# A decoder layer's attention probabilities, turned by VectorE's 32x32 block transposes and a way over DRAM instead of by TensorE

## The chip, the cores and the metric

The kernel runs on one core of a Trainium2 chip. The core has five engines, each with its own queue of instructions that it works through strictly in order: TensorE (PE, matrix products, with the weight loads shown as PEld), VectorE (DVE), ScalarE (ACT), GpSimd (POOL) and SyncE (SP, which here only issues DMA transfers). They wait for each other by semaphores. Data lies in the on-chip memory SBUF (128 partitions), in PSUM (the matrix products' accumulators, in banks of 128 x 512 floats) or in DRAM. The metric is the device time of one execution in microseconds (us); less is better. The kernel before takes 956.22 us, the median of three runs from 954.28 to 958.12.

## The reference

One layer of a hybrid decoder over 1024 tokens with 16 learned meta tokens ahead of them, width 1024, everything in float32:

```python
u = rmsnorm(h, g_pre_mix); z = u @ w_in            # q | k | v | x_rec | y_rec
attn = sliding_window_attention_with_sinks(q, k, v, sinks)   # 8 heads of 64, 2 KV heads, window 128
rec  = gelu(y_rec) * rg_lru(causal_conv4(x_rec))             # a gated linear recurrence over time
h = h + rmsnorm(concat(attn, rec) @ w_out, g_post_mix)
u = rmsnorm(h, g_pre_ffn)
h = h + rmsnorm(relu(u @ w_ff1)**2 @ w_ff2, g_post_ffn)
```

The attention part is the one that the change touches. For a block of 128 query tokens a head looks at 256 keys (its own block and the block before), of which each query may see 128; one more score per head, the sink, takes part in the denominator alone:

```python
s = where(valid, q @ k.T * scale, -1e30)
m = maximum(max(s), sink);  p = exp(s - m);  denom = sum(p) + exp(sink - m)
o = (p / denom) @ v
```

The product with v needs the probabilities with the keys in the partitions, while softmax leaves them with the queries in the partitions. So each 128 x 128 block of probabilities has to be turned.

## The kernel before

Every float32 product is made of three products of rounded parts (a high part and the rest, `hi` and `lo`): `split` writes `hi` with a ScalarE cast (line 96) and `lo` with a VectorE subtraction (line 99), and `mm3` issues the three matmuls (lines 125, 130, 131). Matmuls of that form are most of TensorE's work, in every stage.

The stages in time: load and normalise the tokens and project the first columns (to about 60 us), attention together with the remaining input projections (about 60 to 190 us), the recurrence (LRU; about 190 to 260 us), the output projection, and from about 300 us the feed-forward part.

Attention runs in eight steps, a loop over `j` (4 pairs of heads) and `half` (the first or second 512 query tokens). A step handles two heads `h` and four blocks of 128 queries each:

- `scores(j, half, q)`: for each head 8 matmuls into two PSUM banks of the tag `s` (lines 625, 629); ScalarE copies one half of them to the tile `sn` (line 642), VectorE overwrites it with the other half where the mask says so (line 643), so that each query keeps just the 128 keys it may see; a minimum over the row (line 652), four exponentials with their sums (line 82, the helper `lut`), a reciprocal and a multiplication (lines 660, 661).
- `attend(j, half, sn)`: TensorE turns four 128 x 128 blocks per head through the PSUM tag `pt` (line 675); `split` writes `ph` and `pl` from PSUM; eight `affine_select` on GpSimd (line 680) cut each of them into the two key blocks; 10 + 10 matmuls with v (line 691); the two heads' halves are added (lines 705, 706) into a piece called `flat` of the tile that came in, and split into the operand `at` of the output projection.

`attend` of a step is written behind `scores` of the next one. Between them stands `next_fill()`: one more input projection ("fill"), 48 or 96 matmuls into the two PSUM banks of the tag `acc`, which keep TensorE busy while softmax runs elsewhere. Fills are q, x and y projections; their results leave the banks by ScalarE and VectorE (lines 476 and 479 for q, 490 for x, 747 for y). There are ten fills: eight in the loop, two after the gates of the recurrence.

The order on each engine's queue is not the order of the program text. A planner, run when the kernel is built, simulates the program with its own costs and places each instruction by priority when its inputs are ready in that simulation; fills have their priority put back by `FILL_LAG`, so that they fill holes. What comes out is one fixed list per engine. On the chip each engine keeps to its list and waits where an input is late.

SBUF tiles come from slots: `slot(tag, ...)` takes the next buffer of a tag, and a new tile waits until the earlier tile in its buffer has been used up. The tag `c` has 8 buffers (`bufs`), and attention's `sn`, `ph` and `pl` all lie there: 5 tiles in each step (one `sn`, two `ph`, two `pl`). The PSUM tags have two buffers each.

The recurrence (`gates`, `gather`, `decay`, `recur`, `rec_out`) is a chain through TensorE (gate products, line 817), ScalarE (sigmoid, then exp, tanh, sqrt and gelu, each set with a table load) and VectorE (a scan, line 851). While it runs, TensorE has the last fills and the part of the output projection that needs attention alone (`out_mm` with `kc` 0 to 3); `kc` 4 to 7 need the recurrence.

The issue of nearly all loads is on SP, in one list; it waits at a load whose buffer is not yet free, and what stands behind it waits too.

## Time and profile before

| what | value |
|---|---|
| median of three runs | 956.22 us (954.28 to 958.12) |
| span of the profiled execution | 955.3 us (the page gives no other time for it) |
| TensorE (PE) busy | 943.8 us, 99% |
| VectorE busy | 655.7 us, 69% |
| ScalarE busy | 505.9 us, 53% |
| GpSimd busy | 129.1 us, 14% |
| TensorE transposes of line 675 | 64, first at 80.9 us, last at 175.4 us |
| matmuls with v, line 691 | 87.6 to 185.3 us |
| first gate product, line 817 | 196.6 us |

The profile is one execution recorded by the hardware. A group row gives line, engine, operation, the tile written and the tiles read (buffer numbers left out), the count, and behind the bar the busy time in us, the mean of one in ns and the idle time of the engine ahead of the group with what ended it. A timeline row gives the start in us, the length in us, the engine, the line, the operation and, in brackets, the idle time ahead of it. Matmuls overlap in the array, so the distance between two starts says what one of them costs, not its length.

### The profile page before, as it was taken

The page shows a single profiled execution, that of the slowest core. Times are in us where ns is not written, and L with a number is a line of the kernel's source. Part 1 is how long each engine was busy: PE and PEld are TensorE (multiplying, and loading weights), DVE is VectorE, ACT ScalarE, POOL GpSimd, SP SyncE. Part 2 cuts the span into 40 slices and gives each one's busy share as a digit, 9 for nine tenths or more (in the row PEclk, how much of TensorE's full clock was granted, in tenths as well). Part 3 has the DMA queues.
Part 4 walks back from the last instruction along what each step waited for, and adds up shares of the span by engine and source line. Part 5 has one row for each costly group of instructions (what it writes and reads, how often), then busy time and mean ns, then how long its engine had stood idle before and what let it go on. Part 6 is the DMA issues. An engine that isn't in the chain of part 4 may idle for free.

```text
span 955.3 us, 12432 instructions
## 1 busy us (share of the span) xinstructions
PE 943.8 (99%) x4728; PEld 789.7 (83%) x4728; DVE 655.7 (69%) x845; ACT 505.9 (53%) x854; POOL 129.1 (14%) x189
## 2 busy tenths in 40 slices
PE   9999999999999999999999999999999999999996
PEld 8999999877888878888888888888887788888885
DVE  6567987788856787665644465476667576779893
ACT  7537766568645554444655575654433343446441
POOL 4102563520021100010000000001121100001201
PEclk9999999999999999999999999999999999999999
DMA  8221010204226368674422364334777765647934
GB/s 271 56 67 23 24 45 24 67 23 131 83 109 185 133 220 264 198 253 144 155 89 88 111 203 127 104 113 114 175 180 186 185 199 177 192 139 196 246 65 89
DMA packets 88199, 130.21 MB, mean 136 GB/s; under 512 B 13702, under 2 KB 52630, under 8 KB 88140
## 3 DMA queue, kind: packets, MB, share of 16 engines
q1 hardware_dynamic: 78972, 104.44, 34.0%
q0 software_dynamic: 8880, 24.19, 12.2%
q8 instruction: 37, 0.61, 0.3%
q10 hardware_dynamic: 288, 0.79, 0.2%
q14 instruction: 22, 0.18, 0.1%
HBM read 109.93 MB, written 18.87 MB: 135 GB/s over the span
## 4 chain that ended last, share of the span: by engine, by line
PE 88%; DVE 5%; ACT 3%; DMA 2%; POOL 1%; issue 1%; SPq 0%; DVEq 0%; ACTq 0%; POOLq 0%
PE ps_acc L130 10%; PE ps_acc L131 10%; PE ps_acc L125 10%; PE ps_s L131 6%; PE ps_s L130 6%; PE ps_s L125 6%; PE ps_pt L130 6%; PE ps_pt L131 6%; PE ps_pt L125 6%; PE ps_o L130 5%; PE ps_o L131 5%; PE ps_o L125 5%; ACT c L82 1%; PE ps_o L691 1%; PE ps_acc L282 1%
## 5 line engine op out<-in xcount | busy, mean ns | idle before, releaser
L99 DVE TENSOR_TENSOR ws<-raw,ws 128x1024 fp32r<-128x1024 f32 (+1 forms) x69 | 82.6, 1197 | 76.1 <-ACT ws L96 24.3
L96 ACT CAST ws<-raw 128x1024 fp32r<-128x1024 f32 (+1 forms) x68 | 69.7, 1026 | 87.9 <-PE ps_o L130 23.9
L96 ACT CAST ws<-e 128x1024 fp32r<-128x1024 f32 x41 | 43.0, 1049 | 82.8 <-PE ps_o L130 35.3
L125 PE MATMUL ps_acc<-a,ws 128*128 128x256 f32 (+2 forms) x256 | 85.8, 335 | 0.0
L130 PE MATMUL ps_acc<-a,ws 128*128 128x256 f32 (+2 forms) x256 | 85.5, 334 | 0.0
L131 PE MATMUL ps_acc<-a,ws 128*128 128x256 f32 (+2 forms) x256 | 85.0, 333 | 0.0
L99 DVE TENSOR_TENSOR b<-b,b 128x1024 fp32r<-128x1024 f32 (+2 forms) x50 | 58.9, 1177 | 24.8 <-PE ps_o L130 19.1
L96 ACT CAST b<-b 128x1024 fp32r<-128x1024 f32 (+2 forms) x49 | 49.9, 1019 | 46.4 <-DVE b L996 41.0
L99 DVE TENSOR_TENSOR ws<-e,ws 128x1024 fp32r<-128x1024 f32 x41 | 50.1, 1223 | 32.4 <-ACT ws L96 18.9
L680 POOL TENSOR_SCALAR_AFFINE_SELECT c<-c 128x512 fp32r<-128x512 f32 x64 | 53.6, 858 | 67.6 <-ACT c L96 59.3
L125 PEld LDWEIGHTS ps_acc<-a,ws 128*128 128x128 f32 x256 | 48.3, 189 | 4.7 <-issue 0.2
L131 PEld LDWEIGHTS ps_acc<-a,ws 128*128 128x128 f32 x256 | 48.3, 189 | 4.5
L130 PEld LDWEIGHTS ps_acc<-a,ws 128*128 128x128 f32 x256 | 48.2, 188 | 4.4 <-issue 0.4
L125 PE MATMUL ps_acc<-ws,b 128*128 128x512 f32 (+1 forms) x120 | 46.3, 387 | 1.1 <-ACT ws L96 1.1
L130 PE MATMUL ps_acc<-ws,b 128*128 128x512 f32 (+1 forms) x120 | 46.3, 386 | 0.5 <-DVE ws L99 0.4
L131 PE MATMUL ps_acc<-ws,b 128*128 128x512 f32 (+1 forms) x120 | 46.1, 385 | 0.0
L125 PE MATMUL ps_pt<-ws,b 128*128 128x512 f32 x112 | 44.4, 396 | 0.0
L130 PE MATMUL ps_pt<-ws,b 128*128 128x512 f32 x112 | 44.1, 394 | 0.0
L131 PE MATMUL ps_pt<-ws,b 128*128 128x512 f32 x112 | 44.0, 393 | 0.0
L125 PE MATMUL ps_s<-ws,b 128*128 128x512 f32 x110 | 43.4, 395 | 0.0
L131 PE MATMUL ps_s<-ws,b 128*128 128x512 f32 x110 | 43.3, 394 | 0.0
L130 PE MATMUL ps_s<-ws,b 128*128 128x512 f32 x110 | 43.3, 393 | 0.0
(416 smaller groups left out, 2662.0 us busy)
## 6 DMA issues: line engine op xcount, KB each, us to landing
raw<-in_w_ff_dram SPq DMA_DIRECT2D x61, 512.0 KB, 4.1
e<-in_w_ff_dram SPq DMA_DIRECT2D x45, 512.0 KB, 4.0
a<-in_w_ff_dram SPq DMA_DIRECT2D x12, 512.0 KB, 6.6
s_dram<-a POOLq DMA_DIRECT2D x12, 512.0 KB, 3.7
c<-in_x_dram SPq DMA_DIRECT2D x8, 512.0 KB, 4.0
raw<-in_w_in_dram SPq DMA_DIRECT2D x8, 512.0 KB, 3.7
d<-in_x_dram SPq DMA_DIRECT2D x8, 512.0 KB, 3.3
out_dram<-raw SPq DMA_DIRECT2D x8, 512.0 KB
```

The lines of the kernel that those rows point to most:

```text
L82: ins = nc.scalar.activation(*args, **kwargs).ins
L96: nc.scalar.copy(hi, src)
L99: low = nc.vector.tensor_tensor(lo, src, f32(hi), op=ALU.subtract).ins
L125: ins = nc.tensor.matmul(dst, lh, rh, start=start, stop=False, skip_group_check=True).ins
L130: nc.tensor.matmul(dst, lh, rl, start=False, stop=False, skip_group_check=True)
L131: last_mm[0] = nc.tensor.matmul(dst, ll, rh, start=False, stop=stop, skip_group_check=True).ins.name
L282: last_mm[0] = nc.tensor.matmul(acc[:, :n], w[k // 2][:, kc, :], u[kc][k % 2][:, t0 : t0 + n], start=k == 0 and kc == 0, stop=k == last an ...
L680: nc.gpsimd.affine_select(out=p_[:, :, s], in_=f32(p_[:, :, 0]), pattern=[[0, 4], [g, P]], compare_op=op, fill=0.0, base=0, channel_multip ...
L691: nc.tensor.matmul(po[:, oc : oc + n], v, p_[:, pc : pc + n], start=first and k == 0, stop=last and k == 1, skip_group_check=True,)
```

## The change

`scores` no longer returns `sn`. Behind the multiplication it runs one VectorE transpose per step, which turns each 32 x 32 block of `sn` by itself and writes a new tile `y` of the tag `c`. Four DMAs on SP, one for each group of 32 partitions, write `y` to a DRAM tile `p_dram` (512 KB per step) in such an order of rows that one more DMA on SP, which reads them back with four runs of 1 KB for each partition, puts the turned probabilities into a third tile `pt` of the tag `c`. `attend` takes `pt` in place of `sn`: the 8 TensorE transposes per step and the use of the PSUM tag `pt` go, `split` reads SBUF where it read PSUM, and `flat` now lies in `pt`'s buffer. A step so takes 7 tiles of the 8 buffers of the tag `c`.

```diff
+    p_dram = dpool.tile([8, 4, P, 2 * P], F32, name="p_dram")
+
     def scores(j, half, q):
         ...
-        return sn
-
-    def attend(j, half, sn):
-        flat = sn.rearrange("p a b c -> p (a b c)")
+        y = slot("c", [P, 4, 8, 32])
+        nc.vector.transpose(
+            y,
+            sn.rearrange("p h i k -> p (h i) k")[:, :, 0:P].rearrange(
+                "p n (b k) -> p b n k", b=4
+            ),
+        )
+        dram = p_dram[2 * j + half]
+        for a in range(4):
+            nc.sync.dma_start(
+                dram[a].rearrange("(b k) r -> k b r", b=4),
+                y[32 * a : 32 * a + 32].rearrange("p b n q -> p b (n q)"),
+            )
+        pt = slot("c", [P, 4, 2, 4, 32])
+        nc.sync.dma_start(
+            pt.rearrange("p a h i q -> p a (h i q)"), dram.rearrange("a p r -> p a r")
+        )
+        return pt
+
+    def attend(j, half, pt):
+        flat = pt.rearrange("p a h i q -> p (a h i q)")
         pp = []
         for h in range(2):
 
             ph, pl = (slot("c", [P, 4, 2, P], F32R) for _ in range(2))
-            pt = bank("pt")
-            for i in range(4):
-                nc.tensor.transpose(pt[:, i * P : (i + 1) * P], sn[:, h, i, 0:P], ident)
-            pt = pt.rearrange("p (a b) -> p a b", a=4)
-            split(ph[:, :, 0], pl[:, :, 0], pt)
+            split(
+                *(p_[:, :, 0].rearrange("p i (a q) -> p i a q", a=4) for p_ in (ph, pl)),
+                pt[:, :, h].rearrange("p a i q -> p i a q"),
+            )
```

## The prediction

> **What bounds the kernel now.** I read the page's head and the chain of what ended last, then TensorE's waits in the attention stage, then busy time by stretches of that stage.

> ```profile
> span 955.3 us, 12432 instructions
> PE 943.8 (99%) x4728; PEld 789.7 (83%) x4728; DVE 655.7 (69%) x845; ACT 505.9 (53%) x854; POOL 129.1 (14%) x189
> PE 88%; DVE 5%; ACT 3%; DMA 2%; POOL 1%; issue 1%; SPq 0%; DVEq 0%; ACTq 0%; POOLq 0%
> ```
> ```profile
> PE ps_o L691 <- POOL c L680: 0.3, 1, 0.3
> PE ps_pt L130 <- DVE a L99: 0.2, 1, 0.2
> ```
> ```profile
> 100.00:120.00 20.00, 20.00 (x134) 18.24 (x133) 19.45 (x31) 13.31 (x42) 12.06 (x13) 1.00 0.09 28
> 120.00:140.00 20.00, 20.00 (x156) 19.21 (x155) 17.54 (x30) 13.77 (x45) 12.25 (x18) 1.00 0.15 43
> 160.00:180.00 20.00, 20.00 (x141) 18.49 (x141) 17.24 (x28) 13.13 (x39) 11.83 (x13) 1.00 0.17 53
> ```

> TensorE bounds the whole: 99% busy, 88% of the chain. The second fence holds all its waits between 55 and 262 us, and they are half a microsecond. The third (columns: stretch, length, then busy us with counts of PE, PEld, DVE, ACT, POOL) shows VectorE at 17 to 19.5 us of each 20 in attention. So work taken from TensorE counts in full as long as its next instruction is ready; and the engine that gets the work is nearly full just there.

> **What goes.** 64 TensorE transposes.

> ```profile
> 80.92 0.60 PE L675 MATMUL ps_pt<-ident,c 128*128 128x128 f32 x4
> 81.28 0.37 PE L131 MATMUL ps_acc<-a,ws 128*128 128x272 f32 x1
> 81.49 0.29 PE L125 MATMUL ps_acc<-a,ws 128*128 128x272 f32 x1
> 81.61 0.29 PE L130 MATMUL ps_acc<-a,ws 128*128 128x272 f32 x1
> 172.01 0.39 PE L125 MATMUL ps_acc<-a,ws 128*128 128x512 f32 x1
> 172.25 0.39 PE L130 MATMUL ps_acc<-a,ws 128*128 128x512 f32 x1
> ```

> From the first transpose (80.92) to the second matmul behind them (81.49) pass 0.57 us, of which one matmul of 272 columns has 0.12 (81.49 to 81.61). Four transposes so cost 0.45 us, one 0.11, and 64 of them 7.1 us: the whole gain. A matmul of 512 columns costs 0.23 to 0.24.

> [...]

> **What comes on VectorE.** Eight transposes of 128x1024 float32, of which the trace shows none. Nearest rows:

> ```profile
> L958 DVE TENSOR_SCALAR d<-raw,rs 128x1024 f32<-128x1024 f32 x8 | 6.0, 754 | 12.8 <-POOL rs L176 12.8
> L996 DVE TENSOR_TENSOR b<-a,c 128x1024 f32<-128x1024 f32 x15 | 18.3, 1218 | 1.0 <-PE ps_o L130 0.9
> L851 DVE TENSOR_TENSOR_SCAN c<-b,c 128x1040 f32<-128x1040 f32 x2 | 4.6, 2314 | 0.0
> ```

> Bounds 0.75 and 2.31; I take 1.2, one element after another like the plain two-input row. That is 9.6 us on an engine with 0.5 to 2.8 us free in each 20. A gain below nothing is excluded: it is added work. `split` reads SBUF, not PSUM; the row for PSUM (below, 681) and SBUF operations of 512 columns (729) bound it at 0.7, so nothing changes there.

> **What comes on DMA.** Per step four writes of 128 KB and one read of 512 KB, all issued by SP.

> ```profile
> s_dram<-a POOLq DMA_DIRECT2D x12, 512.0 KB, 3.7
> e<-s_dram SPq DMA_DIRECT2D x8, 512.0 KB, 4.4
> ws<-ws POOLq DMA_DIRECT2D x2, 36.0 KB, 2.0
> 185.82 0.50 SPq L865 DMA_DIRECT2D raw<-in_w_out_dram  x1
> ```

> An issue takes 0.5 us, so the four writes 2.0; the last lands after 2.0 (the 36 KB row) to 3.7 us, the read after 4.4. From the transpose to `pt` pass 8.5 to 10.5 us; I take 9. SP's list now has weight loads behind these DMAs, but those have many microseconds in hand, as have the reads of steps 0 to 6: in the built lists `attend` of a step comes 13 to 25 us behind its transpose. Only the last step's read (and the last `w_out` loads behind it) is near the path. Without that cover each step would cost its 9 us.

> **What it does to the lists.** The built program of the changed kernel gives each engine's order. Two things tighten it. Five tiles of `c` per step became seven of eight buffers: from step 4 on `sn` of every step lies in the buffer of the step before it, so a step's scores cannot be copied out of PSUM before the previous step's transpose is done. And the PSUM banks of a fill are emptied by ScalarE and VectorE instructions that stand in their lists behind whole pieces of attention. I walked the lists from 80.9 us (equal until there), starting each instruction when its engine and inputs are free, with these durations:

> ```profile
> L82 ACT ACTIVATE c<-c,negm 128x129 f32<-128x129 f32 x64 | 25.0, 395 | 3.7 <-DVE negm L652 3.5
> L642 ACT COPY c<-ps_s 128x256 f32<-128x256 f32 x32 | 10.5, 373 | 2.6 <-PE ps_s L629 2.5
> L643 DVE COPY_PREDICATED c<-above,ps_s 128x256 f32<-128x256 int32 x32 | 13.0, 448 | 0.6 <-ACT c L642 0.2
> L652 DVE TENSOR_REDUCE negm<-c 128x4 f32<-128x516 f32 x16 | 11.0, 685 | 0.5
> L661 DVE TENSOR_TENSOR c<-c,rden 128x512 f32<-128x512 f32 x16 | 11.7, 729 | 0.4
> L706 DVE TENSOR_TENSOR c<-ps_o,c 64x512 f32<-64x512 f32 x16 | 11.0, 686 | 3.1 <-ACT c L705 2.8
> L705 ACT COPY c<-ps_o 64x512 f32<-64x512 f32 x16 | 9.3, 581 | 9.6 <-PE ps_o L691 9.3
> L99 DVE TENSOR_TENSOR c<-ps_pt,c 128x512 fp32r<-128x512 f32 x16 | 10.8, 681 | 0.1
> L476 ACT ACTIVATE b<-ps_acc x8: 591/592/594, 106.3 to 152.1; 64x512 fp32r<-64x512 f32 x8
> ```

> *Wait A, 6.2 us.* TensorE ends step 0's v-products at 108.0 (its list summed). Next stands a fill whose bank is emptied behind step 2's softmax: exponentials of the second head end at 108.2, then reciprocal and multiplication 0.9, the new transpose 1.2, two additions 1.4, a cast 0.6, two copies of line 476 1.2 and a VectorE subtraction 0.7: 114.2.

> *Waits B, 5.6 us.* Step 1's selects (0.8), and four times the low half of a fill's weights, 1.2 us on VectorE behind attention work (0.4, 1.4, 1.2, 1.8).

> *Wait C, 7.6 us.* The list of TensorE near the end of attention reads:

> ```
> scores step 6, second head | v step 4 | scores step 7, first head (two banks) |
> scores step 7, second head | v step 5 | fill y(2) x24 | ... v step 6 ... | gates | v step 7
> ```

> There is no fill between these. The second head of step 7 needs a bank of the first, which is copied only when `sn`'s buffer is free, that is after step 6's transpose. Behind step 4's last v-product run a copy 0.6, an addition 0.7, the reduction 0.7, exponentials 1.6, reciprocal and multiplication 0.9, a low part 0.7, the transpose 1.2, the copy 0.4 and the masked copy 0.4: 7.2, of which TensorE has 1.1 of work: 6.1. Step 5's selects add 1.5.

> *Wait D, 7.4 us.* The fill y(2) needs the bank of y(1), emptied by VectorE behind step 7's whole softmax and its transpose: after the last scores two copies 0.7, mask 0.8, reduction 0.7, exponentials 1.6, multiplication 0.9, addition 0.7, transpose 1.2, low part 0.7, copy 0.7 and some 2 of latency and queueing: 10; TensorE has 2.5.

> Sum 26.8. My clock leaves out what changes of shape cost TensorE: summed in the same way the kernel before has its first gate product at 192.7, and the trace at 196.62. These 3.9 us shorten the waits: 22.9.

> *The recurrence, 6.0 us.*

> ```profile
> 196.62 0.43 PE L817 MATMUL ps_s<-b,e 64*128 64x348 f32 x1
> 213.33 1.28 ACT L82 ACT_TABLE_LOAD   x1
> 244.16 2.04 ACT L82 ACTIVATE c<-c 128x1040 f32<-128x1040 f32 x2
> 256.79 0.68 DVE L99 TENSOR_TENSOR b<-b,b 128x512 fp32r<-128x512 f32 x1
> 259.78 0.40 PE L125 MATMUL ps_pt<-a,b 128*128 128x512 f32 x1
> ```

> From the last sigmoid (213.3) to the operand of `kc` 6 (256.8) pass 43.5 us, and TensorE uses it at 259.78: 3 us in hand. In the changed list fills 1 and 2 come before the gates, not behind them, so TensorE has 12.3 us less work from the last gate product to `kc` 6. ScalarE's list also has the casts of `w_out` earlier, between sigmoids, which delays the gates' end by 3 and spares 6 to 7 behind it. 12.3 less cover, plus 3, less the 3 in hand, less 6.3: 6.0.

> Sum: -7.1 + 22.9 + 6.0 = +21.8 on the span of 955.3: 977.1. The median of the runs stands 0.9 above that span; forecast 978.0. Behind 300 us nothing changes but small shifts of the plan.

> **Rivals.** *Hidden after all, 949.* If each of A to D shrinks to nothing because ScalarE and VectorE run ahead of their lists, only the 7.1 us remain: 956.2 - 7.1 = 949. For it: 0.5 us of waits today with the same planner. Against it: C and D are chains of fixed instructions with no fill between. It turns faster only when A to D and the tail come to less than 7.1 of my 28.9 us.

> *Half of the waits, 964.* If the walk counts too much: 956.2 - 7.1 + 14.5 = 964.

> *The clock, 985.* At the start the trace shows slow matmuls:

> ```profile
> 1.51 5.06 PE L308 MATMUL ps_acc<-ws 128*128 128x512 f32 x11 [1.51 <-DVE base_e L562]
> ```

> That is 0.46 us each, twice the 0.23 above, for 5.06 us: 2.5 us lost. If an idle TensorE falls back to that speed, A, C and D cost 2.5 us more each: 985, less what later waits swallow. [...]

> *Slow transpose or slow scratch, 988.* At 2.31 us the transpose adds 1.1 in A, C, D and up to three of B's steps (6 us), and a `pt` late by 4 in the last step adds its 4: 988.

> **How the numbers follow.** Forecast case (969 to 983) 0.48; clock 0.22; slow transpose or scratch 0.13; half of the waits 0.09; no change, where waits and gain cancel, 0.04; hidden 0.04. The range 962 to 998 leaves out some 0.1 below and 0.05 above. A measurement of this kernel can tell 0.5% (4.8 us) from no change: faster 0.04, same 0.05, slower 0.91.

> **What would show it.** Right: line 668 at about 1.2 us; TensorE idle gaps of 5 to 8 us near 110, 195 and 205 us, released by VectorE; VectorE above 18 of 20 us before them; the first gate product at about 220 us (196.6 before), two fills now standing ahead of it; last `pt` read landing 9 us behind its transpose. Wrong: TensorE without gaps there, or gaps ended by DMA.

## The result, and the profile after

The changed kernel takes 996.13 us (median; 995.20 to 997.48) beside 955.94 for the kernel before (here the median of four runs): a ratio of 1.0423 with a 95% interval of 1.0405 to 1.0441, some 40 us more. The forecast was 978.0. The profiled execution took 995.54 us, 2.1 more than its span.

The head of the page of the changed kernel, with the granted clock in 40 slices of 24.8 us, and its chain of what ended last:

```profile
span 993.4 us, 12428 instructions
...
PE 955.5 (96%) x4664; PEld 796.9 (80%) x4664; DVE 669.8 (67%) x853; ACT 507.3 (51%) x854; POOL 127.6 (13%) x189
...
PEclk9999799968999999999999999999999999999999
...
PE 85%; DVE 6%; ACT 4%; issue 2%; DMA 2%; POOL 0%; DVEq 0%; SPq 0%; ACTq 0%; POOLq 0%
```

TensorE has 64 instructions less and is busy 11.7 us longer (955.5 against 943.8), and it idles 37.9 us of the span against 11.5. The digits of the clock say why both can be: in three of the slices (99 to 124 and 199 to 248 us) the granted clock is below nine tenths.

TensorE's waits from 60 to 340 us (total, times, longest):

```profile
PE ps_s L627 <- DVE c L645: 10.8, 2, 6.0
PE ps_acc L125 <- DVE b L479: 5.9, 1, 5.9
PE ps_pt L125 <- ACT b L96: 4.7, 1, 4.7
PE ps_acc L125 <- DVE b L765: 4.6, 1, 4.6
PE ps_s L835 <- ACT c L82: 1.3, 1, 1.3
PE ps_pt L131 <- DVE b L99: 0.8, 1, 0.8
PE ps_o L835 <- DVE c L724: 0.4, 1, 0.4
```

Where the kernel before had half a microsecond of waits, there are five gaps of 4.6 to 6.0 us, at 104, 115, 197, 210 and 292 us, and no DMA releases any of them. One of them in TensorE's timeline, with the matmuls on both sides:

```profile
196.87 0.28 PE L631 MATMUL ps_s<-b,b 128*128 128x256 f32 x1
196.99 0.28 PE L627 MATMUL ps_s<-b,b 128*128 128x256 f32 x1
197.11 0.28 PE L631 MATMUL ps_s<-b,b 128*128 128x256 f32 x1
203.41 0.58 PE L627 MATMUL ps_s<-b,b 128*128 128x256 f32 x1 [6.03 <-DVE c L645]
203.79 0.41 PE L631 MATMUL ps_s<-b,b 128*128 128x256 f32 x1
204.00 0.41 PE L627 MATMUL ps_s<-b,b 128*128 128x256 f32 x1
204.22 0.41 PE L631 MATMUL ps_s<-b,b 128*128 128x256 f32 x1
```

Ahead of the gap a 256-column matmul costs 0.12 us (196.87 to 196.99), behind it 0.21 (204.00 to 204.22). The same place in four stretches of 3.41 us (busy time of PE, PEld, DVE, ACT, POOL with counts, then the granted clock, the DMA share, GB/s):

```profile
195.46:198.87 3.41, 1.92 (x16) 1.68 (x14) 3.16 (x7) 2.43 (x10) 0.00 (x0) 1.00 0.56 141
198.87:202.28 3.41, 0.00 (x0) 0.00 (x0) 3.20 (x6) 2.15 (x7) 2.04 (x3) 1.00 0.07 16
202.28:205.70 3.42, 2.29 (x10) 2.21 (x10) 2.07 (x4) 1.36 (x8) 3.34 (x7) 0.50 0.63 153
205.70:209.11 3.41, 3.31 (x16) 3.20 (x16) 2.57 (x6) 1.92 (x9) 0.74 (x2) 0.50 0.50 154
```

The clock is halved at 202.28, when a whole stretch has passed without a matmul, and it stays so while TensorE works again. From 60 to 340 us the clock is halved in five stretches (106.7 to 113.5, 120.4 to 127.2, 202.3 to 219.3, 236.4 to 243.2, 294.4 to 301.3). Summed over stretches of 2 us, busy time times what the clock lacks of 1 comes to 15.8 us of work lost.

So the span's 38.1 us more are made up of 26.4 of idle TensorE and 11.7 of busy TensorE, and the 11.7 of -7.1 (the transposes that went), 15.8 (slow clock) and 3.0 that is left over and not explained.

The new work itself, from the groups and from the DMA issues (KB each, us to landing):

```profile
L668 DVE STREAM_TRANSPOSE c<-c 128x1024 f32<-128x1024 f32 x8 | 9.9, 1243 | 0.2
```
```profile
p_dram<-c SPq DMA_DIRECT2D x32, 128.0 KB, 1.9
c<-p_dram SPq DMA_DIRECT2D x8, 512.0 KB, 3.7
```

VectorE's transpose takes 1.24 us, where the prediction took 1.2; that is 0.16 us for each 128 x 128 float32.

### The profile page after: what moved, and what is told of

It is laid out like the page before. It is cut to its first block, busy times and chain, and to the rows that moved or that the text cites. A ratio compares the mean times of both kernels' runs of the same rounds, so it can differ in the third digit from the quotient of the medians.

```text
span 993.4 us, 12428 instructions
## 1 busy us (share of the span) xinstructions
PE 955.5 (96%) x4664; PEld 796.9 (80%) x4664; DVE 669.8 (67%) x853; ACT 507.3 (51%) x854; POOL 127.6 (13%) x189
## 4 chain that ended last, share of the span: by engine, by line
PE 85%; DVE 6%; ACT 4%; issue 2%; DMA 2%; POOL 0%; DVEq 0%; SPq 0%; ACTq 0%; POOLq 0%
PE ps_acc L125 10%; PE ps_acc L130 10%; PE ps_acc L131 10%; PE ps_s L131 6%; PE ps_s L125 6%; PE ps_pt L125 6%; PE ps_s L130 6%; PE ps_pt L130 6%; PE ps_pt L131 5%; PE ps_o L130 5%; PE ps_o L125 5%; PE ps_o L131 5%; ACT c L82 2%; PE ps_o L709 1%; PE ps_acc L282 1%
## 5 line engine op out<-in xcount | busy, mean ns | idle before, releaser
L99 DVE TENSOR_TENSOR ws<-raw,ws 128x1024 fp32r<-128x1024 f32 (+1 forms) x69 | 82.4, 1194 | 73.4 <-ACT ws L96 24.6
L125 PE MATMUL ps_acc<-a,ws 128*128 128x256 f32 (+2 forms) x256 | 88.2, 344 | 10.5 <-DVE b L479 5.9
L130 PE MATMUL ps_acc<-a,ws 128*128 128x256 f32 (+2 forms) x256 | 87.2, 341 | 0.0
L131 PE MATMUL ps_acc<-a,ws 128*128 128x256 f32 (+2 forms) x256 | 87.1, 340 | 0.0
L99 DVE TENSOR_TENSOR b<-b,b 128x1024 fp32r<-128x1024 f32 (+2 forms) x50 | 58.9, 1179 | 25.6 <-PE ps_o L130 19.6
L99 DVE TENSOR_TENSOR ws<-e,ws 128x1024 fp32r<-128x1024 f32 x41 | 50.1, 1223 | 32.6 <-ACT ws L96 19.3
L698 POOL TENSOR_SCALAR_AFFINE_SELECT c<-c 128x512 fp32r<-128x512 f32 x64 | 49.0, 792 | 118.0 <-ACT c L96 115.7
L125 PEld LDWEIGHTS ps_acc<-a,ws 128*128 128x128 f32 x256 | 50.5, 197 | 16.0 <-DVE b L479 6.0
L131 PEld LDWEIGHTS ps_acc<-a,ws 128*128 128x128 f32 x256 | 50.2, 196 | 5.0 <-issue 0.2
L130 PEld LDWEIGHTS ps_acc<-a,ws 128*128 128x128 f32 x256 | 50.3, 196 | 4.6 <-issue 0.2
L130 PE MATMUL ps_acc<-ws,b 128*128 128x512 f32 (+1 forms) x120 | 46.3, 386 | 0.3 <-DVE ws L99 0.3
L125 PE MATMUL ps_acc<-ws,b 128*128 128x512 f32 (+1 forms) x120 | 46.2, 386 | 0.2 <-ACT ws L96 0.2
L131 PE MATMUL ps_acc<-ws,b 128*128 128x512 f32 (+1 forms) x120 | 46.1, 385 | 0.0
L125 PE MATMUL ps_pt<-ws,b 128*128 128x512 f32 x112 | 44.2, 395 | 0.0
L130 PE MATMUL ps_pt<-ws,b 128*128 128x512 f32 x112 | 44.2, 395 | 0.0
L131 PE MATMUL ps_pt<-ws,b 128*128 128x512 f32 x112 | 44.0, 393 | 0.0
L125 PE MATMUL ps_s<-ws,b 128*128 128x512 f32 x110 | 43.5, 396 | 0.0
L130 PE MATMUL ps_s<-ws,b 128*128 128x512 f32 x110 | 43.3, 393 | 0.0
L131 PE MATMUL ps_s<-ws,b 128*128 128x512 f32 x110 | 43.3, 393 | 0.0
## 6 DMA issues: line engine op xcount, KB each, us to landing
raw<-in_w_ff_dram SPq DMA_DIRECT2D x61, 512.0 KB, 4.2
e<-in_w_ff_dram SPq DMA_DIRECT2D x45, 512.0 KB, 4.4
a<-in_w_ff_dram SPq DMA_DIRECT2D x12, 512.0 KB, 6.6
s_dram<-a POOLq DMA_DIRECT2D x12, 512.0 KB, 4.1
c<-in_x_dram SPq DMA_DIRECT2D x8, 512.0 KB, 4.2
raw<-in_w_in_dram SPq DMA_DIRECT2D x8, 512.0 KB
c<-p_dram SPq DMA_DIRECT2D x8, 512.0 KB, 3.7
```

Source lines behind the costliest of these rows:

```text
L99: low = nc.vector.tensor_tensor(lo, src, f32(hi), op=ALU.subtract).ins
L125: ins = nc.tensor.matmul(dst, lh, rh, start=start, stop=False, skip_group_check=True).ins
L130: nc.tensor.matmul(dst, lh, rl, start=False, stop=False, skip_group_check=True)
L131: last_mm[0] = nc.tensor.matmul(dst, ll, rh, start=False, stop=stop, skip_group_check=True).ins.name
L698: nc.gpsimd.affine_select(out=p_[:, :, s], in_=f32(p_[:, :, 0]), pattern=[[0, 4], [g, P]], compare_op=op, fill=0.0, base=0, channel_multip ...
```

## The experiments

All losses below are (ratio - 1) x 955 us, since each group of runs had its own runs of the kernel before. Busy and clock are TensorE's from 60 to 340 us, one row of the windows for each kernel; the kernel before has 279.50 of 280. "Fill ahead" is read from the built lists: the projection matmuls that stand in TensorE's list between the first scores of all and step 7's first scores, at 0.23, 0.125 and 0.118 us for 512, 272 and 256 columns, the distances between two starts in the trace of the kernel before. In every kernel 48 of them (5.7 us) still belong to the projections ahead of the ten fills, so that only the differences between kernels count.

| kernel | ratio, 95% | loss, us | busy | clock | fill ahead, us |
|---|---|---|---|---|---|
| before | 1 | 0 | 279.50 | 1.00 | 67.6 |
| changed | 1.0423 (1.0405 to 1.0441) | 40.4 | 251.36 | 0.92 | 95.4 |
| e1 before, no turning | 0.9989 (0.9980 to 0.9998) | -1.1 | 277.43 | 1.00 | 70.3 |
| e2 no scratch | 1.0198 (1.0183 to 1.0213) | 18.9 | 266.57 | 0.96 | 79.3 |
| e3 `y` in e | 1.0440 (1.0422 to 1.0459) | 42.0 | 250.67 | 0.93 | 95.4 |
| e4 filler | 1.0423 (1.0400 to 1.0446) | 40.4 | 257.21 | 0.94 | 95.4 |
| e5 scratch unread | 1.0405 (1.0387 to 1.0423) | 38.7 | 249.97 | 0.94 | 95.4 |
| e6 before + VectorE transposes | 0.9996 (0.9987 to 1.0005) | -0.4 | 279.75 | 1.00 | 67.6 |
| e7 four score banks | 1.0270 (1.0253 to 1.0287) | 25.8 | 261.20 | 0.95 | 82.5 |
| e8 and two steps behind | 1.0298 (1.0282 to 1.0313) | 28.5 | 258.72 | 0.95 | 76.0 |
| e9 turn per head | 1.0234 (1.0219 to 1.0249) | 22.3 | 261.49 | 0.97 | 88.5 |
| e10 per head, four banks | 1.0067 (1.0050 to 1.0084) | 6.4 | 270.48 | 0.99 | 69.0 |
| e11 e10 without scratch | 1.0050 (1.0033 to 1.0067) | 4.8 | 273.10 | 0.99 | 66.4 |
| e12 e10, two steps behind | 1.0117 (1.0102 to 1.0132) | 11.2 | 270.44 | 0.98 | 73.3 |

### e1: what the transposes were worth

```diff
-            pt = bank("pt")
-            for i in range(4):
-                nc.tensor.transpose(pt[:, i * P : (i + 1) * P], sn[:, h, i, 0:P], ident)
-            pt = pt.rearrange("p (a b) -> p a b", a=4)
-            split(ph[:, :, 0], pl[:, :, 0], pt)
+            split(ph[:, :, 0], pl[:, :, 0], sn[:, h, :, 0:P])
```

> The kernel before with its 64 TensorE transposes taken out and nothing put in their place: the casts of attend read the probabilities as they stand, so the output of attention is left unturned, and the time is that of the kernel before less the transposes. Step 1 of the prediction (0.11 us for each transpose): about 7 us less, 949. [...] If the loss of the changed kernel came from the lists of the engines being built anew whenever this stage is touched, and not from what was put in: no gain at all or a loss, 956 to 980, with new waits of TensorE between 100 and 220 us.

953.76 us, 1.1 less (0.2 to 1.9), and not 7. The page's head:

```profile
span 951.9 us, 12300 instructions
...
PE 940.1 (99%) x4664; PEld 783.9 (82%) x4664; DVE 657.6 (69%) x845; ACT 507.9 (53%) x854; POOL 134.2 (14%) x189
```

TensorE is busy 3.7 us less than before and not 7.1, so the other matmuls take 3.4 more, and from 60 to 340 us it idles 2.6 us where the kernel before idles 0.5. By the trace of the kernel before, the 64 transposes do hold some 7 us. But the lists are built anew without them, and most of that comes back as waits and as dearer neighbours; which neighbours, the runs do not tell. So what there was to gain, with the lists as this planner builds them, was about 1 us.

### e6: VectorE's transposes by themselves

```diff
+        y = slot("e", [P, 4, 8, 32])
+        nc.vector.transpose(y, sn.rearrange("p h i k -> p (h i) k")[:, :, 0:P].rearrange(
+                "p n (b k) -> p b n k", b=4))
         return sn
```

> The kernel before, TensorE transposes and all, with the eight VectorE transposes of 128x1024 added behind the softmax, into a free buffer of tag e that nobody reads. Nothing is left out. Theory V (VectorE is nearly full in attention, so 9.9 us on it come back as waits of TensorE): 960 to 966. Rival (VectorE's added work is hidden, the loss comes from what depends on it and from the lists): 954 to 958.

It took 953.73 us: no difference. These are the group of the new instructions, and VectorE (the third busy time) in two stretches:

```profile
L666 DVE STREAM_TRANSPOSE e<-c 128x1024 f32<-128x1024 f32 x8 | 9.8, 1229 | 0.0
```
```profile
100.00:120.00 20.00, 20.00 (x138) 18.44 (x137) 19.75 (x30) 12.98 (x38) 7.08 (x11) 1.00 0.18 54
160.00:180.00 20.00, 20.00 (x136) 18.28 (x135) 18.39 (x27) 11.74 (x37) 10.75 (x12) 1.00 0.15 41
```

VectorE is busy for 18.4 to 19.75 of 20 us and TensorE loses nothing: theory V falls. Busy for 19.75 of 20 us, VectorE was not late: TensorE, busy for all 20.00, did not wait for it in that stretch. Nobody reads these transposes, so the run prices VectorE's time alone; the 1.24 us by which a transpose that is read lengthens the chain, and its effect on the lists, it leaves out.

### e2 and e5: the way over DRAM, taken out, and taken out of the dependences alone

e2 leaves out the writes, the reads and `pt`; e5 keeps them all and lets `attend` read `y`:

```diff
-        return pt
+        return y.rearrange("p b (h i) q -> p b h i q", h=2)
```

> The changed kernel without the way over DRAM: the eight transposes on VectorE stay, attend reads their result directly (so the blocks stand in the wrong places and the output of attention is wrong), and the 32 writes, the 8 reads and the tile that the reads fill are left out: six tiles of c per step, not seven. Theory A (the softmax chain and the buffers make the waits, the DMAs do not): the waits that come from sn's buffer and from fill banks behind the softmax stay in the main, one or two of them shrink: 980 to 996. Rival B (the way over DRAM, 9 us from transpose to pt and the queue of SyncE behind it, is on the path): all gaps of 4.6 to 6 us go, 949 to 955.

> The changed kernel with all its DMAs, but attend takes the result of VectorE's transpose itself and not what the way over DRAM brings back (so the blocks stand in the wrong places and the output of attention is wrong; the reads land in a tile that nobody uses). TensorE's order differs from the changed kernel's in 6 of 4587 rows, VectorE's in 2, the others not at all: so this takes away the wait for DRAM at run time and keeps the orders of the lists. Theory L (the orders make the loss: fills drawn forward, softmax chains left bare at the end): 990 to 997, with the gaps at 104, 115, 197 and 210 us as they were. Rival W (at run time something waits for the way over DRAM, 9 us from transpose to pt): 955 to 975.

e2 measured 972.68 us and e5 993.12 us. Without the DMAs 21.5 of the 40.4 us go and 18.9 stay. With the DMAs in place and no product waiting for what they bring back, 1.7 go (38.7 against 40.4, with intervals that overlap). So rival W of e5 falls, and of e2 neither theory was right. The waits of e5:

```profile
PE ps_s L627 <- DVE c L645: 10.7, 2, 6.0
PE ps_acc L125 <- DVE b L479: 5.7, 1, 5.7
PE ps_acc L125 <- DVE b L765: 5.6, 1, 5.6
PE ps_pt L125 <- ACT b L96: 4.7, 1, 4.7
```

These are the gaps of the changed kernel. The DMAs are hardly waited for while the program runs: by the releasers that the trace of the changed kernel names, TensorE, VectorE, ScalarE and GpSimd together wait 5.7 us for one between 60 and 300 us (ScalarE, 4.4 and 1.3), and TensorE never; none of TensorE's waits in e5 names one either. What is left between e5 and e2 is the order of the lists. Ahead of step 7's scores stand 95.4 us of fill in the changed kernel and in e5, and 79.3 in e2, and behind them there is little left to stand in. How the DMAs move the lists is not shown: in e5 the products no longer hang on the read, and the order still came out as in the changed kernel but for six rows. TensorE's built lists from step 7's first scores on (S scores as step.part, with one part for each PSUM bank that is filled, V products with v of a step, T transposes, F fill, G gates, with the number of matmuls of each):

```
before:     S7.0 x2 | V5 x9 | S7.0 x2 | S7.1 x4 | F x8 | T x4 | F x10 | T x4 | F x5 | S7.2 x4 | S7.3 x4 | F x14 | V6 x1 | F x11 | V6 ...
changed:    S7.0 x4 | S7.1 x4 | S7.2 x4 | V5 x1 | S7.3 x4 | V5 x19 | F x28 | V6 x1 | ...
e2:         S7.0 x4 | S7.1 x4 | F x46 | V5 x2 | F x7 | S7.2 x3 | V5 x18 | S7.2 x1 | S7.3 x4 | F x65 | V6 ...
```

In the changed kernel nothing stands between S7.1 and S7.2, nor between V5 and the fill whose bank is emptied behind step 7's softmax: the gaps at 197 and 210 us.

### e3: the result of the transpose in another buffer

```diff
-        y = slot("c", [P, 4, 8, 32])
+        y = slot("e", [P, 4, 8, 32])
```

> The changed kernel with the result of VectorE's transpose in a buffer of tag e (one of its two is free in attention) in place of c: the orders of TensorE, ScalarE and GpSimd stay as they are, instruction by instruction; c has six tiles per step for eight buffers. Theory A1 (one buffer for the scores of all steps makes the wait before step 7's second head): that wait of 6.0 us goes or falls below 2, and with it the slow clock behind it: 984 to 990. Rival A2 (the order of the lists alone makes the waits, whatever the buffers): 994 to 997, the four gaps as before.

It took 994.91 us, like the changed kernel, and the wait is 6.1 us as before. A1 falls and A2 stands: the shared buffer of `sn` was not what held step 7 back.

### e4: filler in two gaps

```diff
+    def warm(n, name):
+        ...                                  # two lines left out
+        spare = bank("pt")
+        for _ in range(n):
+            ins = nc.tensor.matmul(spare, vk[0][:, 0, :],
+                vk[0].rearrange("p a b -> p (a b)")[:, :512],
+                start=True, stop=True, skip_group_check=True).ins
+            behind(name, ins)
+            name = ins.name
```

Ten of these matmuls stand behind the fill of `q` 2 and twenty behind S7.1.

> The changed kernel with 30 useless matmuls of 512 columns on TensorE: 10 (2.3 us at full clock) behind the last matmul of the fill before the gap at 104 us, and 20 (4.6 us) behind the scores of step 7's first head, before the gap at 197 us. All other instructions stay in their orders. Theory C (an idle TensorE falls to half its clock and that is a cost of its own, some 15 us over six gaps): the spacing of 256-column matmuls behind the two filled gaps is 0.12 us and not 0.21, and the time is the same or up to 5 us less, 991 to 996, although 6.9 us of work are added. Rival D (slow matmuls behind the gaps come from data, ports or DMA traffic of these places, not from idleness): the spacing stays at 0.21, time 996 to 1003.

It took 994.12 us: the same ratio as the changed kernel, with 6.9 us of work more. These are TensorE around 197 us, and three stretches there:

```profile
196.36 4.72 PE L618 MATMUL ps_pt<-b 128*128 128x512 f32 x20
202.54 0.39 PE L641 MATMUL ps_s<-b,b 128*128 128x256 f32 x1 [1.47 <-DVE c L659]
202.77 0.28 PE L645 MATMUL ps_s<-b,b 128*128 128x256 f32 x1
202.89 0.28 PE L641 MATMUL ps_s<-b,b 128*128 128x256 f32 x1
```
```profile
198.24:201.65 3.41, 2.84 (x13) 2.02 (x11) 3.38 (x6) 2.11 (x5) 2.18 (x4) 1.00 0.01 2
201.65:205.06 3.41, 1.67 (x11) 1.32 (x11) 1.84 (x4) 1.41 (x7) 3.41 (x7) 1.00 0.63 154
205.06:208.48 3.42, 3.42 (x16) 3.42 (x17) 2.80 (x6) 1.93 (x8) 0.52 (x1) 0.50 0.51 153
```

Behind the filled gap the scores run at 0.12 us; then the clock falls all the same at 205.06, behind a stretch in which TensorE was busy for 1.67 of 3.41 us. At 104 us the filler left 2.4 us idle, and the clock was halved for 3.4 us and not for 6.8. So far theory C holds: with the gap at 197 us filled, the scores of this place run at 0.12 us and not at the 0.21 of the changed kernel. What it saves in time can't be told from nothing here, since the chains behind the gaps wait for ScalarE and VectorE.

### e7 and e8: four banks for the scores, and a longer distance

```diff
-                sp_ = bank("s", (P, 2, 256))
+                sp_ = bank(("s", "pt")[bp], (P, 2, 256))
```

(both with `y` in e); e8 also keeps two steps waiting:

```diff
-            if prev is not None:
-                attend(*prev)
-            prev = (j, half, sn)
-    attend(*prev)
+            late.append((j, half, sn))
+            if len(late) > 2:
+                attend(*late.pop(0))
+    for step in late:
+        attend(*step)
```

> The changed kernel with the PSUM banks of tag pt, which attention no longer uses, given to the scores: four banks in place of two, so a step's second head needs no copy of its first; and the result of the transpose in tag e. Nothing is left out. Theory B (the score banks make the gaps at 104 and 197 us, 10.8 us of waiting and some 5 of slow clock): both go, 978 to 984. Rival L (the softmax chains stand bare because the fills are spent early: 95 of some 110 us of fill stand ahead of step 7's scores, 68 of 103 in the kernel before): the wait moves to the next matmul that needs the chain, 988 to 997.

> As the kernel with four score banks, and attend of a step stands two steps behind its scores in place of one, so that two steps of products are left for TensorE behind the last scores. Nothing is left out. Theory L (what is missing is work that can stand between a step's scores and the end of its softmax, transpose and way over DRAM): the gaps of steps 6 and 7 go, the tail of the recurrence (4.7 us and its slow clock) stays: 962 to 975. Rival B (banks and buffers, not the distance): as with four score banks alone, within 3 us of it. Rival P (the planner spends whatever cover there is): 985 to 997.

They took 980.13 and 982.74 us. The waits of e7:

```profile
PE ps_acc L125 <- DVE b L479: 6.5, 1, 6.5
PE ps_acc L125 <- DVE b L765: 4.3, 1, 4.3
PE ps_pt L125 <- ACT b L96: 3.9, 1, 3.9
```

The two waits for a scores bank (10.8 us) are gone, as theory B had it, and 14.6 us with them; the fill banks and the recurrence still wait. e8 is no better: its new gap of 4.7 us is a product that waits for the selects. Theory L in the form of e8 falls, and rival B (within 3 us of e7) stands: the greater distance between scores and products brought nothing by itself.

### e9 to e12: the turn for each head by itself

```diff
+        y = slot("e", [P, 4, 8, 32])
+        pt = slot("c", [P, 4, 2, 4, 32])
         ...                                  # in the loop over h, behind the multiplication
+            nc.vector.transpose(
+                y[:, :, 4 * h : 4 * h + 4],
+                sn[:, h, :, 0:P].rearrange("p n (b k) -> p b n k", b=4),
+            )
+            for a in range(4):
+                nc.sync.dma_start(
+                    dram[a].rearrange("(b k) r -> k b r", b=4)[:, :, h * P : (h + 1) * P],
+                    y[32 * a : 32 * a + 32, :, 4 * h : 4 * h + 4].rearrange("p b n q -> p b (n q)"),
+                )
+            nc.sync.dma_start(
+                pt[:, :, h].rearrange("p a i q -> p a (i q)"),
+                dram.rearrange("a p r -> p a r")[:, :, h * P : (h + 1) * P],
+            )
```

e9 also has `y` in e, which by e3 makes no difference. e10 adds the four banks of e7; e11 is e10 without the DMAs and with `y` in c, read by `attend` itself; e12 is e10 with the two steps of e8.

> The changed kernel with the turn made for each head by itself: behind each head's softmax a VectorE transpose of 128x512, four writes of 64 KB and a read of 256 KB, in place of one transpose of 128x1024, four writes of 128 KB and a read of 512 KB behind both; the result of the transpose lies in tag e. Nothing is left out; the DMAs are twice as many, of half the size. In the built lists 88.5 us of fill stand ahead of step 7's scores (95.4 in the changed kernel, 67.6 in the kernel before) and 34.9 ahead of the first product (39.2 and 23.0). Theory L (the longer way from scores to products draws the fills forward and leaves the last chains bare): one of the gaps at 197 and 210 us goes or both shrink, 978 to 990. Rival Q (SyncE's queue and the number of DMAs are the price): 996 to 1005.

> The turn per head and four PSUM banks for the scores together. Nothing is left out. In the built lists 69.0 us of fill stand ahead of step 7's scores, near the 67.6 of the kernel before. Theory L: the gaps at 104, 197 and 210 us go with their slow clock; what stays is the fill bank emptied behind the softmax (5.6 to 6.5 us in every run so far) and the tail of the recurrence (4 to 5): 962 to 972. Rival B (the banks alone did it): 978 to 982, as with four banks alone.

> The turn per head with four score banks, and without the way over DRAM: attend reads the result of VectorE's transposes itself (so the blocks stand in the wrong places and the output of attention is wrong), and the writes, the reads and their tile are left out. In the built lists 66.4 us of fill stand ahead of step 7's scores and 25.1 ahead of the first product, like the 67.6 and 23.0 of the kernel before. Theory L (the way over DRAM costs by what it does to the lists, and VectorE's turn itself nothing): 950 to 955, no gap over 3 us. Rival (some 6 us of loss stay with VectorE's part of the turn): 958 to 962.

> The turn per head, four score banks, the whole way over DRAM, and attend two steps behind the scores. Nothing is left out. In the built lists 73.3 us of fill stand ahead of step 7's scores (69.0 with attend one step behind) and 42.2 ahead of the first product (34.6). Theory L by the fills: not better than one step behind, 961 to 972. Rival (the gaps that are left, a product that waits for the selects at 111 us among them, are covered by the second step): 954 to 960.

They took 977.04, 961.25, 960.06 and 966.75 us. e9 has twice the DMA issues of the changed kernel and loses 18 us less: rival Q falls, and e9 lies 1 us under the range of theory L. e10 keeps the whole way over DRAM and VectorE's turn, and 34 of the 40.4 us are gone. Its rival B falls, and it lies 1 us under the range of theory L: the waits for a fill bank and at the recurrence's end, which theory L expected to stay, shrank to under 2 us. The head and the waits of e10:

```profile
PE 940.5 (98%) x4664; PEld 784.4 (82%) x4664; DVE 670.9 (70%) x861; ACT 506.0 (53%) x854; POOL 126.4 (13%) x189
```
```profile
PE ps_o L710 <- POOL c L699: 4.2, 1, 4.2
PE ps_acc L125 <- ACT d L490: 3.3, 2, 2.1
```

TensorE is busy for 940.5 us, as in e1; one gap over 3 us is left (a product that waits for the selects, at 111 us), and the slow clock takes 1.6 us and not 15.8. Without the way over DRAM e11 loses 1.6 us less (4.8 against 6.4, with intervals that overlap), so in this form that way costs little or nothing. But e11 missed its theory by 5 to 10 us and lies in the range of its rival, by which some 6 us stay with VectorE's part of the turn: its fills stand like those of the kernel before, and it is 4.8 us slower. By e6 VectorE's added time alone doesn't cost that; the longer chain and the changed lists were not told apart, so the last 5 us stay open. Nor does the fill ahead of step 7 order the runs by itself: e9 has more of it than e7 and e8 and loses less, and e1 has more than e10 and loses nothing. No form with the turn on VectorE beat the kernel before.

## Why the prediction was right or wrong

The direction, the mechanism of the gaps and most of their places were right; the sum was 16 us short on the span (21.8 forecast, 38.1 measured). The 996 us lie above the forecast case and above every rival that the prediction priced, the highest at 988. They lie within its range, but the range's upper end, 998, stands for no case that the prediction worked out; that the range held is in part luck. Step by step:

- *What goes, 7.1 us "in full".* The rows were right, the conclusion not: by e1 the transposes are worth 1 us when the lists are built anew without them.
- *VectorE, 1.2 us.* Measured 1.24 and, by e6, free where it was feared, on a nearly full VectorE (18.4 to 19.75 of 20 us).
- *DMA, 9 us hidden for all but the last step.* In the last step 8.9 us pass from the start of the transpose (212.01) to the cast that waits for `pt` (220.95), and by e5 the wait at run time costs 1.7 us, which the intervals do not tell from nothing. The prediction took the built lists as they were and did not ask what the DMAs had done to them, so its waits A to D hold that effect without naming it: e5 against e2 puts some 20 us of the loss there.
- *Waits A to D, 26.8.* A measured 5.9 for 6.2, C 6.0 for 7.6 (its selects added nothing), D 4.6 for 7.4. B (5.6 of small waits) did not come, and there is a gap of 4.7 us at 104 us that the walk missed; that the two nearly cancel is luck. ScalarE's timeline there:

```profile
98.16 0.19 ACT L82 ACTIVATION_READ_ACCUMULATOR c<-c,negm 128x1 f32 x1
104.00 1.04 ACT L96 CAST ws<-raw 128x1024 fp32r<-128x1024 f32 x1 [5.65 <-issue]
104.95 1.13 ACT L96 CAST c<-c 128x512 fp32r<-128x512 f32 x2
105.99 0.64 ACT L644 COPY c<-ps_s 128x256 f32<-128x256 f32 x2
```

  The cast of a fill's weights stands ahead of the copies that free step 2's score banks. It starts at 104.00, while TensorE's last matmul of the running fill (103.75 to 104.15) runs, and its list entry waits for TensorE to release a buffer of `ws`; the profile names no releaser. The load that it reads was not late: it was issued at 93.47, and these loads land after 3.5 us. So, as far as the trace shows, ScalarE waited for the end of a fill, and TensorE then for ScalarE. In e2 and in e7, whose lists are others, the gap is gone.
- *The reason given for C*, that `sn`'s shared buffer keeps the scores in PSUM, fell with e3: the same softmax chain is waited for, but because of its place in the lists and of the two score banks (e7), not because of the buffer.
- *The recurrence, 6.0.* 0.8 and 4.7 us of waits at 280 and 292, 5.5 in all; the first gate product came at 230.35 and not at 220, and by then the slow clock had taken some 11 us of TensorE's work, half of its 4.65, 5.80 and 11.24 us of busy time in the first three slow stretches.
- *The sum.* Idle time was forecast at 28.9 and came to 26.4. What failed is that the sum has no term for the clock. The rival named it, with 2.5 us at three gaps, 7.5 in all; it was 15.8 over five slow stretches, since after each fall the clock stayed down for 6.8 to 17.1 us, and TensorE worked for most of that time. A, C and D came 4.7 us shorter than the walk had them; whether the 3.9 us taken off for changes of shape are the reason, no run shows.
- *What would show it.* VectorE above 18 of 20 us ahead of the gaps was wrong. Two stretches around the gaps:

```profile
100.00:120.00 20.00, 10.79 (x58) 9.56 (x56) 13.11 (x22) 9.40 (x29) 6.46 (x10) 0.83 0.39 106
200.00:220.00 20.00, 11.89 (x42) 10.42 (x43) 16.34 (x24) 10.63 (x30) 9.35 (x14) 0.57 0.38 102
```

  VectorE is busy for 13.1 and 16.3 us, so it is not full over 20 us. Inside a gap it can be: in the stretch from 198.87 us, shown with the result, it is busy for 3.20 of 3.41 us. There TensorE waits for the last of a row of instructions on VectorE and ScalarE, and VectorE's share of them runs nearly without a break.

## What to carry to other kernels

Where a planner builds each engine's list, new steps between a producer and its consumer can cost less by their own time than by what they move in the lists. So compare the built lists before and after, see what is left to stand behind the last chains, and cut the new step into pieces that can start early (per head here: 18 us). Give resources that the change frees (two PSUM banks here, 15 us) to whatever now waits. And price every forecast gap of several microseconds on TensorE with the slow clock behind it: in the changed kernel it cost 15.8 us of TensorE's work, beside five gaps of 26.0 us in all.
